# Row sums on one core: one contiguous run of 105 rows per partition in place of eight blocks of 16

## The chip, the core and the metric

The kernel runs on one core of a Trainium2 chip. The metric is device time in microseconds (us) of one execution; lower is better. Two engines compute here: VectorE (DVE in the profile) and ScalarE (ACT). SyncE (SP) issues the loads and the last store, ScalarE the other store. The data moves on the core's 16 DMA engines.

## The reference

```python
batch, seq, dim = 32, 512, 1024
x = np.random.randn(batch, seq, dim).astype(np.float32)
out = np.sum(x, axis=-1).astype(np.float32)      # (32, 512)
```

There are 16,384 rows of 1,024 floats (4 KB each). 67.1 MB are read, 64 KB are written, and every element is used in one addition.

## The kernel before

The rows are spread over 128 partitions, 128 rows to each. They are cut into eight blocks of 2,048 rows; in a block, partition p holds 16 neighbouring rows (64 KB), so a block is one contiguous stretch of 8 MB, and a partition's 64 KB follow those of the partition before it. `sums` is a tile of 128 x 128 floats that gathers one sum for each row: column g*16 + q is row q of block g.

The order of work is written out by hand (`manual_schedule`); each engine runs its own list in program order, with semaphore waits between the engines. All loads are issued by SP into tiles of a pool with three buffers (`inpool`), so a load waits until the tile three before it has been read. `rows` issues a load and the work on it: either one reduction of all its rows on VectorE (`vec`, L141), or row by row, some on VectorE (`halves`, L155: one half of the row is added to the other with a running sum) and some on ScalarE (`act`, L168: a copy with a running sum into PSUM).

1. The first load takes the first 7 rows (28 KB) per partition of the last block. It is moved by `issue_first_load_at_entry` to the program's entry, ahead of the barrier that starts the engines.
2. Blocks 0 to 6 follow, each one load of 16 rows (64 KB per partition, 8 MB in all). Blocks 0 to 5 are reduced by one VectorE instruction each. Block 6 is split: 9 rows to VectorE and 7 to ScalarE. The load of block 1 is held by hand until the reduction of the first 7 rows is done ("no descriptors of later loads while the first ones start").
3. The rest of the last block comes in loads of 6 rows, 2 rows, and the last row in two pieces of 536 and 488 elements (L222, L223).
4. Two stores (L191): `sums` of blocks 0 to 6 from ScalarE's queue, held until the load of two rows has landed, and the 16 sums of the last block from SP's queue at the very end. In the first one every partition writes seven pieces of 64 bytes, in the second one piece of 64 bytes.
5. `wait_for_the_store_at_the_clear` lets the last store run beside the barrier at the end; only GpSimd's clearing of the semaphores waits for it. `order_waits` arranges which of several waits an instruction itself carries.

Of the kernel before, what the change touches and what calls it, by code (L numbers as in the profile page):

```python
# [100 lines left out]
@with_exitstack  # L101
def kernel(
    ctx: ExitStack,
    tc: tile.TileContext,
    x: bass.AP,
    out: bass.AP,
):
    nc = tc.nc
    nc.at_finalize(issue_first_load_at_entry)
    nc.at_finalize(order_waits)  # L110
    nc.at_finalize(wait_for_the_store_at_the_clear)
    fp32 = mybir.dt.float32
    P = 128
    batch, seq, dim = x.shape
    rows = batch * seq
    J = rows // P
    BIG = 16


    x_g = x.flatten_outer_dims().rearrange("(g p j) d -> g p j d", p=P, j=BIG)  # L120
    out_v = out.rearrange("b s -> (b s)").rearrange("(g p j) -> p g j", p=P, j=BIG)

    def rows_from(j, n):
        return x_g[j // BIG, :, j % BIG : j % BIG + n, :]

    last = J // BIG - 1
    FIRST = 7
    pieces = (536, 488)  # L130

    with (
        tc.tile_pool(name="in", bufs=3) as inpool,
        tc.tile_pool(name="unread", bufs=4, space=bass.MemoryType.PSUM) as upool,
        tc.tile_pool(name="stage", bufs=1) as stpool,
        tc.manual_schedule(),
    ):
        sums = stpool.tile([P, J], fp32)

        def vec(dst, src):  # L140
            return nc.vector.tensor_reduce(  # L141
                out=dst, in_=src, axis=mybir.AxisListType.X, op=mybir.AluOpType.add
            )

        def hold(inst, until, reason):
            tc.add_manual_dep(
                inst.ins,
                until.ins.name,
                mybir.DependencyInfo(mybir.DependencyClass.Sync, mybir.DependencyReason.DATA),
                reason=reason,  # L150
            )

        def halves(dst, src):
            n = src.shape[-1] // 2
            return nc.vector.tensor_tensor_reduce(  # L155
                out=src[:, :n],
                in0=src[:, :n],
                in1=src[:, n:],
                scale=1.0,
                scalar=0.0,  # L160
                op0=mybir.AluOpType.add,
                op1=mybir.AluOpType.add,
                accum_out=dst,
            )

        def act(dst, src, n):
            unread = upool.tile([P, dim], fp32)
            nc.scalar.activation(  # L168
                out=unread[:, :n],
                in_=src,  # L170
                func=mybir.ActivationFunctionType.Copy,
                accum_out=dst,
            )

        sums_of = []

        def rows(t, a, n, j, n_act, pairs=False):
            nv = n - n_act
            block = t[:, a * dim : (a + n) * dim].rearrange("p (n d) -> p n d", d=dim)
            load = nc.sync.dma_start(out=block, in_=rows_from(j, n))  # L180
            if pairs:
                for q in range(nv):
                    sums_of.append(halves(sums[:, j + q : j + q + 1], block[:, q, :]))
            else:
                sums_of.append(vec(sums[:, j : j + nv], block[:, :nv, :]))
            for q in range(nv, n):
                act(sums[:, j + q : j + q + 1], block[:, q, :], dim)
            return load

        def store(eng, g0, g1):  # L190
            return eng.dma_start(  # L191
                out=out_v[:, g0:g1],
                in_=sums[:, g0 * BIG : g1 * BIG].rearrange("p (g j) -> p g j", j=BIG),
            )


        j = last * BIG
        t = inpool.tile([P, BIG * dim + 4], fp32)
        rows(t, 0, FIRST, j, 0)
        first = sums_of[-1]  # L200
        for g in range(last):
            t = inpool.tile([P, BIG * dim + 4], fp32)
            if g < last - 1:
                load = rows(t, 0, BIG, g * BIG, 0)
            else:
                rows(t, 0, BIG, g * BIG, 7, pairs=True)
            if g == 1:
                hold(load, first, "no descriptors of later loads while the first ones start")

        t = inpool.tile([P, BIG * dim + 4], fp32)  # L210
        rows(t, FIRST, 6, j + FIRST, 2, pairs=True)
        two = rows(t, FIRST + 6, 2, j + FIRST + 6, 1, pairs=True)
        a = BIG - 1

        j += a
        c, width = pieces
        whole = t[:, a * dim + c : BIG * dim + 2]
        nc.vector.memset(whole[:, width + 1 :], 0.0)  # L220
        part = t[:, a * dim : a * dim + c]
        nc.sync.dma_start(out=part, in_=rows_from(j, 1)[:, 0, :c])  # L222
        nc.sync.dma_start(out=whole[:, 1 : width + 1], in_=rows_from(j, 1)[:, 0, c:])  # L223
        hold(store(nc.scalar, 0, last), two, "its packets come behind those of the loads")
        halves(whole[:, :1], part)
        halves(sums[:, j : j + 1], whole)
        store(nc.sync, last, last + 1)


# [28 lines left out]
```

## Time and profile before

| | before |
|---|---|
| median of 3 runs | 161.61 us (161.48 to 161.74) |
| span of the profiled execution | 160.3 us, 1.3 us less than the median; its own whole time is not listed apart from the runs, and the median stands for it |
| VectorE busy | 120.6 us (75%), 40 instructions |
| ScalarE busy | 11.9 us (7%), 21 instructions |
| DMA, SP's queue (q1) | 1,872 packets, 67.12 MB, 97.7% of 16 engines' span |
| DMA, ScalarE's queue (q10) | 912 packets, 0.06 MB, 0.4% |
| mean rate over the span | 419 GB/s |

Busy time is the time in which an engine executes; its share is of the span. A DMA packet is one piece that one DMA engine moves, here one partition's contiguous bytes of one load or store, and each DMA adds 16 small ones that raise its semaphore. The share of a queue is the time that its packets took, as a share of 16 engines over the span.

### The profile page before, as it was taken

What the parts mean: (1) busy time and instruction counts of PE and PEld (TensorE: products, weight loads), DVE (VectorE), ACT (ScalarE), POOL (GpSimd) and SP (SyncE); (2) the same over time, 40 slices, a digit from 0 to 9 for tenths busy, and PEclk for the clock granted to TensorE, in tenths of its full rate; (3) what the DMA queues carried; (4) which work ended last, traced back from release to release, by engine and by line L of the source; (5) the groups of instructions that cost most, each with busy time, mean ns of one, the idle gap of its engine ahead of it and who ended that gap; (6) DMA issues with size and microseconds to landing.
All of it is one profiled execution on the core that took longest, in us unless ns stands there. A gap on an engine that the chain in (4) does not pass through costs nothing.

```text
span 160.3 us, 132 instructions
## 1 busy us (share of the span) xinstructions
DVE 120.6 (75%) x40; ACT 11.9 (7%) x21; POOL 0.2 (0%) x4
## 2 busy tenths in 40 slices
DVE  0029600499986999679995999949999499994955
ACT  3000000000000000000000000000000000003993
POOL 0000000000000000000000000000000000000000
DMA  8999999899799699699699699796996996996994
GB/s 300 386 491 523 392 392 523 376 409 523 327 458 523 294 491 523 262 523 523 262 523 523 262 523 441 343 523 278 507 523 262 523 523 262 523 523 264 423 384 123
DMA packets 2784, 67.18 MB, mean 419 GB/s; under 512 B 1248, under 2 KB 1376, under 8 KB 1504
## 3 DMA queue, kind: packets, MB, share of 16 engines
q1 hardware_dynamic: 1872, 67.12, 97.7%
q10 hardware_dynamic: 912, 0.06, 0.4%
HBM read 67.11 MB, written 0.07 MB: 419 GB/s over the span
## 4 chain that ended last, share of the span: by engine, by line
DMA 71%; DVE 27%; SPq 1%; issue 0%; DVEq 0%
DMA t<-in_x_dram 71%; DVE sums L141 26%; SPq L180 0%; SPq L222 0%; DVE t L155 0%; DVEq L253 0%
## 5 line engine op out<-in xcount | busy, mean ns | idle before, releaser
L141 DVE TENSOR_REDUCE sums<-t 128x16 f32<-128x16384 f32 (+1 forms) x7 | 110.9, 15848 | 33.8 <-DMA t<-in_x_dram 33.8
L168 ACT ACTIVATE unread<-t 128x1024 f32<-128x1024 f32 x10 | 10.1, 1012 | 145.3 <-DMA t<-in_x_dram 145.3
L155 DVE CUSTOM_DVE_ANT_0 t<-t 128x512 f32<-128x512 f32 (+2 forms) x16 | 9.6, 656 | 4.1 <-DMA t<-in_x_dram 4.0
L168 ACT ACTIVATION_READ_ACCUMULATOR unread<-t 128x1 f32 x10 | 1.9, 187 | 0.0
L168 ACT ACT_TABLE_LOAD x1 | 1.3, 1283 | 0.8 <-PEq L242 0.8
L155 DVE DVE_READ_ACCUMULATOR2_ANT sums<- 128x1 f32 x15 | 1.3, 84 | 0.0
L242 POOL MEMSET const-bfloat16-1.0<- 128x1 bf16 x1 | 0.1, 101 | 0.0
L242 POOL MEMSET const-uint8-127<- 128x1 uint8 x1 | 0.1, 101 | 0.0
L242 POOL MEMSET const-float32-0.0<- 128x1 f32 x1 | 0.1, 98 | 0.2 <-issue 0.2
L242 POOL MEMSET const-float32-1.0<- 128x1 f32 x1 | 0.1, 98 | 0.0
L155 DVE DVE_READ_ACCUMULATOR2_ANT t<- 128x1 f32 x1 | 0.1, 83 | 0.0
L220 DVE MEMSET t<- 128x1 f32 x1 | 0.1, 59 | 0.0
## 6 DMA issues: line engine op xcount, KB each, us to landing
t<-in_x_dram SPq DMA_DIRECT2D x1, 3584.0 KB, 11.0
t<-in_x_dram SPq DMA_DIRECT2D x1, 3072.0 KB, 29.0
t<-in_x_dram SPq DMA_DIRECT2D x1, 1024.0 KB, 31.1
t<-in_x_dram SPq DMA_DIRECT2D x1, 268.0 KB, 31.4
t<-in_x_dram SPq DMA_DIRECT2D x1, 244.0 KB, 31.4
t<-in_x_dram SPq DMA_DIRECT2D x7, 41.1
out_dram<-sums ACTq DMA_DIRECT2D x1, 56.0 KB, 2.1
out_dram<-sums SPq DMA_DIRECT2D x1, 8.0 KB, 1.4
```

What stands on the lines that cost most here:

```text
L141: return nc.vector.tensor_reduce(out=dst, in_=src, axis=mybir.AxisListType.X, op=mybir.AluOpType.add)
L155: return nc.vector.tensor_tensor_reduce(out=src[:, :n], in0=src[:, :n], in1=src[:, n:], scale=1.0, scalar=0.0, op0=mybir.AluOpType.add, op ...
L168: nc.scalar.activation(out=unread[:, :n], in_=src, func=mybir.ActivationFunctionType.Copy, accum_out=dst,)
L220: nc.vector.memset(whole[:, width + 1 :], 0.0)
L242: nc = _bacc.Bacc("TRN2", target_bir_lowering=False, num_devices=1)
```

## The change

The rows are assigned to partitions in another way, and the loads, the stores and one wait change with it. Each partition now holds 7 rows of a first block (rows 0 to 895 of x), 105 neighbouring rows of a second one (420 KB per partition) and 16 rows of a last block. The 105 rows come in seven loads of 15 rows (60 KB per partition), which start 420 KB apart from one partition to the next. The last block is unchanged in shape, but all of its 16 rows are loaded at the end, in loads of 7, 6, 2 rows and the two pieces of the last row. Each block has a store of its own: 28 bytes per partition after the first reduction, from ScalarE's queue; 420 bytes per partition, held as before until the load of two rows has landed; and 64 bytes per partition at the end. The hold on the second large load is gone.

```diff
-    BIG = 16
-    x_g = x.flatten_outer_dims().rearrange("(g p j) d -> g p j d", p=P, j=BIG)
-    out_v = out.rearrange("b s -> (b s)").rearrange("(g p j) -> p g j", p=P, j=BIG)
+    HEAD, BIG, LOADS = 7, 15, 7
+    RUN = BIG * LOADS
+    LAST = J - HEAD - RUN          # 16
+    def block(first, n):
+        lo, hi = first * P, (first + n) * P
+        return (
+            x_r[lo:hi, :].rearrange("(p j) d -> p j d", j=n),
+            out_r[lo:hi].rearrange("(p j) -> p j", j=n),
+        )
+    x_h, out_h = block(0, HEAD)
+    x_m, out_m = block(HEAD, RUN)
+    x_l, out_l = block(HEAD + RUN, LAST)
...
-        rows(t, 0, FIRST, j, 0)                      # j = 112: part of the last block
-        first = sums_of[-1]
-        for g in range(last):
-            t = inpool.tile([P, BIG * dim + 4], fp32)
-            if g < last - 1:
-                load = rows(t, 0, BIG, g * BIG, 0)
+        rows(t, 0, x_h, 0, 0)
+        nc.scalar.dma_start(out=out_h, in_=sums[:, :HEAD])
+        for g in range(LOADS):
+            t = inpool.tile([P, size], fp32)
+            src = x_m[:, g * BIG : (g + 1) * BIG, :]
+            if g < LOADS - 1:
+                rows(t, 0, src, HEAD + g * BIG, 0)
             else:
-                rows(t, 0, BIG, g * BIG, 7, pairs=True)
-            if g == 1:
-                hold(load, first, "no descriptors of later loads while the first ones start")
+                rows(t, 0, src, HEAD + g * BIG, 7, pairs=True)
...
-        rows(t, FIRST, 6, j + FIRST, 2, pairs=True)
-        two = rows(t, FIRST + 6, 2, j + FIRST + 6, 1, pairs=True)
+        rows(t, 0, x_l[:, :7, :], j, 3, pairs=True)
+        rows(t, 7, x_l[:, 7:13, :], j + 7, 2, pairs=True)
+        two, _ = rows(t, 13, x_l[:, 13:15, :], j + 13, 1, pairs=True)
...
-        hold(store(nc.scalar, 0, last), two, "its packets come behind those of the loads")
+        early = nc.scalar.dma_start(out=out_m, in_=sums[:, HEAD : HEAD + RUN])
+        hold(early, two, "its packets come behind those of the loads")
...
-        store(nc.sync, last, last + 1)
+        nc.sync.dma_start(out=out_l, in_=sums[:, j:])
```

In the instruction lists this gives SP one more load; ScalarE one more store, which stands ahead of its table load and all its activations, and 13 activations for 10; VectorE one reduction of 7 and six of 15 rows (for six of 16), and 19 `halves` for 16.

More of the change, by code (lines that the diff above doesn't have):

```diff
@@ L116 @@
     J = rows // P
-    BIG = 16
-    x_g = x.flatten_outer_dims().rearrange("(g p j) d -> g p j d", p=P, j=BIG)
-    out_v = out.rearrange("b s -> (b s)").rearrange("(g p j) -> p g j", p=P, j=BIG)
[L123 to L129, printed above, removed]
+    HEAD, BIG, LOADS = 7, 15, 7
+    RUN = BIG * LOADS
+    LAST = J - HEAD - RUN
+    assert LAST == 16
+    x_r = x.flatten_outer_dims()
+    out_r = out.rearrange("b s -> (b s)")
+    def block(first, n):
[7 more added lines that the diff above has]
+    x_l, out_l = block(HEAD + RUN, LAST)
     pieces = (536, 488)
@@ L173, in act, with rows @@
             )
-        sums_of = []
-        def rows(t, a, n, j, n_act, pairs=False):
+        def rows(t, a, src, j, n_act, pairs=False):
+            n = src.shape[1]
             nv = n - n_act
-            block = t[:, a * dim : (a + n) * dim].rearrange("p (n d) -> p n d", d=dim)
-            load = nc.sync.dma_start(out=block, in_=rows_from(j, n))
+            part = t[:, a * dim : (a + n) * dim].rearrange("p (n d) -> p n d", d=dim)
+            load = nc.sync.dma_start(out=part, in_=src)
@@ L181, in rows @@
             if pairs:
                 for q in range(nv):
-                    sums_of.append(halves(sums[:, j + q : j + q + 1], block[:, q, :]))
+                    done = halves(sums[:, j + q : j + q + 1], part[:, q, :])
             else:
-                sums_of.append(vec(sums[:, j : j + nv], block[:, :nv, :]))
+                done = vec(sums[:, j : j + nv], part[:, :nv, :])
             for q in range(nv, n):
-                act(sums[:, j + q : j + q + 1], block[:, q, :], dim)
-            return load
@@ L190, in store @@
[L190 to L197, printed above, removed]
-        t = inpool.tile([P, BIG * dim + 4], fp32)
-        rows(t, 0, FIRST, j, 0)
-        first = sums_of[-1]
-        for g in range(last):
-            t = inpool.tile([P, BIG * dim + 4], fp32)
-            if g < last - 1:
-                load = rows(t, 0, BIG, g * BIG, 0)
-            else:
-                rows(t, 0, BIG, g * BIG, 7, pairs=True)
-            if g == 1:
-                hold(load, first, "no descriptors of later loads while the first ones start")
@@ L210 @@
-        t = inpool.tile([P, BIG * dim + 4], fp32)
-        rows(t, FIRST, 6, j + FIRST, 2, pairs=True)
-        two = rows(t, FIRST + 6, 2, j + FIRST + 6, 1, pairs=True)
-        a = BIG - 1
-        j += a
+                act(sums[:, j + q : j + q + 1], part[:, q, :], dim)
+            return load, done
+        size = LAST * dim + 4
+        t = inpool.tile([P, size], fp32)
+        rows(t, 0, x_h, 0, 0)
+        nc.scalar.dma_start(out=out_h, in_=sums[:, :HEAD])
+        for g in range(LOADS):
+            t = inpool.tile([P, size], fp32)
+            src = x_m[:, g * BIG : (g + 1) * BIG, :]
+            if g < LOADS - 1:
+                rows(t, 0, src, HEAD + g * BIG, 0)
+            else:
+                rows(t, 0, src, HEAD + g * BIG, 7, pairs=True)
@@ L218 @@
+        j = HEAD + RUN
+        t = inpool.tile([P, size], fp32)
+        rows(t, 0, x_l[:, :7, :], j, 3, pairs=True)
+        rows(t, 7, x_l[:, 7:13, :], j + 7, 2, pairs=True)
+        two, _ = rows(t, 13, x_l[:, 13:15, :], j + 13, 1, pairs=True)
         c, width = pieces
-        whole = t[:, a * dim + c : BIG * dim + 2]
+        a = LAST - 1
+        whole = t[:, a * dim + c : LAST * dim + 2]
         nc.vector.memset(whole[:, width + 1 :], 0.0)
         part = t[:, a * dim : a * dim + c]
-        nc.sync.dma_start(out=part, in_=rows_from(j, 1)[:, 0, :c])
@@ L223 @@
-        nc.sync.dma_start(out=whole[:, 1 : width + 1], in_=rows_from(j, 1)[:, 0, c:])
-        hold(store(nc.scalar, 0, last), two, "its packets come behind those of the loads")
+        nc.sync.dma_start(out=part, in_=x_l[:, a, :c])
+        nc.sync.dma_start(out=whole[:, 1 : width + 1], in_=x_l[:, a, c:])
+        early = nc.scalar.dma_start(out=out_m, in_=sums[:, HEAD : HEAD + RUN])
+        hold(early, two, "its packets come behind those of the loads")
         halves(whole[:, :1], part)
-        halves(sums[:, j : j + 1], whole)
@@ L227 @@
-        store(nc.sync, last, last + 1)
+        halves(sums[:, J - 1 : J], whole)
+        nc.sync.dma_start(out=out_l, in_=sums[:, j:])
 _INS = ['x']
```

## The prediction

> **What bounds the kernel now.** I read the chain that ended last first. It is this, with start, length and what ran:
>
> ```profile
> 0.00 11.00 DMA t<-in_x_dram
> 11.02 7.63 DVE sums L141
> 18.67 31.00 DMA t<-in_x_dram
> ...
> 66.94 41.09 DMA t<-in_x_dram
> 108.05 17.23 DVE sums L141
> ...
> 126.65 31.45 DMA t<-in_x_dram
> 158.13 0.42 DVE t L155
> ```
>
> The VectorE pieces in it are not a bound. The chain follows each load back to what released its issue, but every load was issued while earlier ones still ran: issued at 66.94, landed at 108.03, 41.09 us for bytes that need 19.5. What is to be seen is that it begins with DMA and ends with DMA and 2.2 us of tail. The waits confirm it: VectorE has only loads to wait for.
>
> ```profile
> DVE sums L141 <- DMA t<-in_x_dram: 33.8, 7, 11.7
> DVE t L155 <- DMA t<-in_x_dram: 4.0, 2, 2.3
> ```
>
> Then the groups by shape (count; busy us, mean ns):
>
> ```profile
> L141 DVE TENSOR_REDUCE sums<-t 128x16 f32<-128x16384 f32 x6 | 103.3, 17220 | 22.8 <-DMA t<-in_x_dram 22.8
> L141 DVE TENSOR_REDUCE sums<-t 128x7 f32<-128x7168 f32 x1 | 7.6, 7619 | 11.0 <-DMA t<-in_x_dram 11.0
> ```
>
> A reduction (17.22) is shorter than the 19.3 to 19.5 between landings. Last the windows from landing to landing; the last two columns are DMA share and GB/s:
>
> ```profile
> 11.02:30.34 19.32, 7.62 (x1) 0.00 (x0) 0.00 (x0) 1.00 1.00 434
> 30.34:49.69 19.35, 17.22 (x2) 0.00 (x0) 0.00 (x0) 1.00 1.00 434
> 49.69:69.05 19.36, 17.22 (x2) 0.00 (x0) 0.00 (x0) 1.00 1.00 433
> 69.05:88.54 19.49, 17.22 (x1) 0.00 (x0) 0.00 (x0) 1.00 1.00 430
> 88.54:108.05 19.51, 17.22 (x2) 0.00 (x0) 0.00 (x0) 1.00 1.01 430
> 108.05:127.53 19.48, 17.22 (x1) 0.00 (x0) 0.00 (x0) 1.00 1.00 431
> ```
>
> The 16 DMA engines are full from about 1 us to the end. The time is their start, 4.19 MB for each engine, and the tail; only what lengthens or shortens that stream counts.
>
> The trace's packet records (read one by one, not through a view) give the price of the stream. An undisturbed 64 KB packet takes 2,418 ns, one of 24 KB 912, one of 8 KB 309: 37.7 ns per 1,024 bytes, and 7.7 ns per packet on top. Eight 64 KB packets and a semaphore packet of 9 ns are 19.35 us, the second and third window above. The last four large loads took 0.14, 0.16, 0.13 and 0.18 us more (19.49, 19.51, 19.48, and 147.06 - 127.53 = 19.53): 0.6 us of slow packets, up to 170 ns each, in the first half of each load. At the start, the first packets begin between 0.99 and 1.95 us, and most of them take 1.50 to 1.86 us where later ones of 28 KB take 1.06.
>
> **The change, part by part,** against the profiled execution: span 160.3 us, and 1.3 us around it up to the median of 161.61, which I leave as they are.
>
> *Bytes and packets.* Each engine reads the same 4.19 MB. There is one load more: 8 packets of 7.7 ns and 9 ns, +0.07 us. A 15-row load is eight packets of 2,418 - 4 x 37.7 = 2,267 ns: 18.15 us per load.
>
> *VectorE and ScalarE.* A 15-row reduction is 7,619 + 8 x (17,220 - 7,619)/9 = 16,150 ns, under 18.15, so VectorE still waits 2.0 us for each load. After the last large load it has 8 rows of 0.61 (nine took 147.06 to 152.57): 4.9 us; ScalarE 7 rows, 7.3 us (147.06 to 154.35). The next load, 7 rows, takes 8 x 1,062 ns = 8.5 us, so both finish first; its 4 and 3 rows (2.5 and 3.1 us) lie within the 7.3 us of the 6-row load. From there on the tail is the one before. Cost zero; without that cover the sixteenth row would push ScalarE by 1.03.
>
> *Buffers and queues.* The third large load waits for the first reduction (18.65), with two loads of 18.15 still queued. The loads of the last block wait for the fifth 15-row reduction: landing 11.0 + 5 x 18.15 = 101.8, end 117.9, while the stream is in the sixth load (to 119.9) and has the seventh behind it. Margin 20 us, cost zero. On ScalarE the new store waits at the head of the queue until 18.65; behind it are the table load (1.28 us, at 0.76 before) and the activations, the first at about 138: zero.
>
> *The first store* is new in the middle of the stream: 8 packets of 28 bytes and one for the semaphore on each engine. The nearest row is q10's: 912 packets, 0.4% of 160.3 us, so 57 per engine in 0.64 us, 11.2 ns each: 9 x 11.2 = 0.10 us. Those ran behind one another with no load between them. The far end: each of the eight stops its engine for as long as a load's last packet takes to become a landing, 0.40 us (157.69 to 158.09 in the records): 3.2 us. The lower end is zero. I take 0.10, the row for small stores. The Trainium skill (DMA: Bandwidth & Descriptors, "Queues, rings and completion order") has an engine alternate between queues packet by packet; no row here shows two queues at once. If a store packet then waits for a load packet each time, the store lands some 18 us late, which nobody waits for, and the sum would be the same.
>
> *The second store* has 128 packets of 420 bytes for 896 of 64. Its old packets ran from 157.87 to 158.60 by the records; the last load's had ended at 157.69, and those of the last store began at 159.43. It stood between the two and touched neither, so I give no gain; at most 0.2 us if it slows the last store's landing.
>
> *The hold removed.* The second large load is issued at about 1.1 us, not at 18.67, behind two issues of 0.36 and 0.33. It brings nothing, since the queue never ran dry. Issues in mid-stream cost nothing that the windows show (lower bound 0). At the start three engines began 0.3 to 0.6 us after the other thirteen, when the first large load was being issued; one more such pause would be +0.3. Or a gain of 0.1, if more is in flight. I take the middle of 0 and 0.3: +0.15.
>
> *The addresses.* This is the large unknown. The 16 engines read 60 KB pieces 420 KB apart instead of one solid 8 MB. Lower bound: the slow packets vanish, -0.6. Upper bound: all seven loads show the worst first packets (170 ns) on every packet: 56 x 0.17 = 9.5 us, unlikely in whole; a plausible end is that all seven run twice as slow as the four slow ones, 7 x 0.3 - 0.6 = +1.5. The nearest rows (434 to 430) are within 1% of each other, so I take zero. The Trainium skill (same page, "Latency and other measured facts", HBM row pitch) reports full rate again where a large power-of-two pitch is padded by 4 KB, or where tiles lie contiguously. The change gives up the second remedy, and 420 KB is no power of two; by the rule its sum would be zero too, or -0.6 if 64 KB steps are what slows the four loads.
>
> Sum: 0.07 + 0.10 + 0.15 = +0.32, 161.93, slightly over 0.2%.
>
> **Rivals.** *The slow packets go away.* Place: the four windows of 19.48 to 19.53. For it: they are slow only in half of each load, which looks like addresses, and the 24 KB and 8 KB packets have none. Against: the first three windows have the same layout and are fast. -0.6 + 0.32 gives 161.33; with no start cost 161.18. It decides as soon as more than half of the 0.6 goes.
> *The wide pitch is slower.* For it: every load now touches the whole 55 MB rather than 8 MB. Against: the solid blocks show no cost at new 8 MB stretches. At +0.3 to +1.5: 162.2 to 163.4, middle 162.7.
> *The first store stalls the engines.* 8 packets at 0.05 to 0.2 us beyond their price: 162.3 to 163.5, middle 162.7. Only the second and third landing would be late.
> *Nothing happens:* start and store are hidden, +0.07, 161.68.
>
> **How the numbers follow.** Small costs as summed: 0.37; slow packets gone: 0.25; pitch 0.20; store 0.08; nothing 0.10. About 0.2% (0.32 us, so 161.29 to 161.93) is what a measurement of this kernel can tell from no change. The first case lies on that edge: 0.26 of it slower, 0.11 same. The second: 0.23 faster, 0.02 same. The pitch and the store: 0.28 slower. Nothing: 0.08 same, 0.02 faster. Faster 0.25, same 0.21, slower 0.54. The range reaches from the second case to the middle of the third and fourth: 161.15 to 162.8; the first case's own range is 161.7 to 162.3.
>
> **What would show it.** Right: landings 18.15 to 18.3 us apart at 430 to 434 GB/s, the first at 11.0 to 11.3, the tail after the last landing 2.2 us, a span near 160.6. The first rival shows as seven windows all at 434. The third as windows all under 428; the fourth as one or two slow windows after 18.7 only. I am wrong altogether if VectorE or ScalarE is late after the last large load, if the tail shrinks by more than 0.2, or if the first landing moves by more than 0.5.

## The result and the profile after

| | before | after |
|---|---|---|
| median time | 161.55 us (6 runs, 161.43 to 161.86) | 162.18 us (6 runs, 162.04 to 162.26) |
| span, median of the runs | 159.9 us (76 runs of all comparisons) | 160.0 us |
| time less span, mean | 1.78 us (the same 76 runs) | 2.17 us |

The ratio is 1.0034, 95% interval [1.0021, 1.0046]; a second comparison (b0 below) gave 162.29 against 161.62, 1.0042 [1.0030, 1.0054]. The changed kernel is 0.6 us slower.

The third row of the table is the main finding. Each run lists its time and its span, and they differ by a constant of the kernel, with a scatter of about 0.03 us. The change lengthens the span a little and the time around it by 0.4 us. The page shown for before (160.3 us) is of an execution longer than most: of the 76 runs listed, 6 have a span of 160.3 or more. The 1.3 us that the prediction took to lie around the span was that profile's span set against the median of other runs.

The windows of the profile after, from landing to landing (busy times; then granted clock, DMA share, GB/s):

```profile
0.00:11.13 11.13, 0.00 (x0) 0.00 (x0) 0.20 (x4) 1.00 1.03 418
11.13:29.31 18.18, 7.62 (x2) 1.28 (x1) 0.00 (x0) 1.00 1.00 433
29.31:47.43 18.12, 16.15 (x1) 0.00 (x0) 0.00 (x0) 1.00 1.00 434
47.43:65.60 18.17, 16.18 (x2) 0.00 (x0) 0.00 (x0) 1.00 1.00 433
65.60:83.70 18.10, 16.13 (x1) 0.00 (x0) 0.00 (x0) 1.00 1.00 434
83.70:101.86 18.16, 16.15 (x2) 0.00 (x0) 0.00 (x0) 1.00 1.00 433
101.86:120.00 18.14, 16.15 (x1) 0.00 (x0) 0.00 (x0) 1.00 1.00 434
...
157.87:160.08 2.21, 0.42 (x2) 0.00 (x0) 0.00 (x0) 1.00 0.04 4
```

The large loads run at full rate, 18.1 to 18.2 us each as costed, and the tail of 2.2 us is the old one. Only the first landing is later: the first reduction starts at 11.13 for 11.02. The waits and the groups show that VectorE still waits for loads alone:

```profile
DVE sums L148 <- DMA t<-in_x_dram: 31.6, 7, 11.1
DVE t L162 <- DMA t<-in_x_dram: 10.4, 3, 4.8
```

```profile
L148 DVE TENSOR_REDUCE sums<-t 128x15 f32<-128x15360 f32 x6 | 96.9, 16153 | 20.5 <-DMA t<-in_x_dram 20.5
```

The reduction is the predicted 16.15 us. Nothing in the page explains 0.6 us; its span is even 0.2 shorter than that of the page before. The one row that turned out to matter is VectorE's count of instructions, in the busy times of the pages, here of before and of after:

```profile
DVE 120.6 (75%) x40; ACT 11.9 (7%) x21; POOL 0.2 (0%) x4
```

```profile
DVE 116.1 (73%) x46; ACT 15.2 (10%) x27; POOL 0.2 (0%) x4
```

### The profile page after: what moved, and what is told of

The parts are those of the page before. It is cut to its first block, busy times and chain, and to the rows that moved or that the text cites. A ratio compares the mean times of both kernels' runs of the same rounds, so it can differ in the third digit from the quotient of the medians.

```text
span 160.1 us, 148 instructions
## 1 busy us (share of the span) xinstructions
DVE 116.1 (73%) x46; ACT 15.2 (10%) x27; POOL 0.2 (0%) x4
## 4 chain that ended last, share of the span: by engine, by line
DMA 76%; DVE 20%; SPq 1%; issue 0%; DVEq 0%
DMA t<-in_x_dram 76%; DVE sums L148 20%; SPq L186 1%; SPq L224 0%; DVE t L162 0%; DVEq L256 0%
## 5 line engine op out<-in xcount | busy, mean ns | idle before, releaser
L148 DVE TENSOR_REDUCE sums<-t 128x15 f32<-128x15360 f32 (+1 forms) x7 | 104.5, 14934 | 31.6 <-DMA t<-in_x_dram 31.6
L175 ACT ACTIVATE unread<-t 128x1024 f32<-128x1024 f32 x13 | 13.2, 1013 | 123.3 <-DMA t<-in_x_dram 123.3
L162 DVE CUSTOM_DVE_ANT_0 t<-t 128x512 f32<-128x512 f32 (+2 forms) x19 | 11.5, 661 | 10.6 <-DMA t<-in_x_dram 10.4
L175 ACT ACTIVATION_READ_ACCUMULATOR unread<-t 128x1 f32 x13 | 2.4, 186 | 0.0
## 6 DMA issues: line engine op xcount, KB each, us to landing
out_dram<-sums ACTq DMA_DIRECT2D x1, 3.5 KB, 21.8
```

Of the source, the lines that this page charges most:

```text
L148: return nc.vector.tensor_reduce(out=dst, in_=src, axis=mybir.AxisListType.X, op=mybir.AluOpType.add)
L162: return nc.vector.tensor_tensor_reduce(out=src[:, :n], in0=src[:, :n], in1=src[:, n:], scale=1.0, scalar=0.0, op0=mybir.AluOpType.add, op ...
L175: nc.scalar.activation(out=unread[:, :n], in_=src, func=mybir.ActivationFunctionType.Copy, accum_out=dst,)
```

## The experiments

Every experiment was timed in five rounds beside the kernel before. "Around" is the time less the span, the mean over the runs; spans are medians.

| experiment | VectorE instructions on the page | time | span | around | ratio to before, 95% |
|---|---|---|---|---|---|
| a1 after, first store left out | 46 | 162.34 | 160.15 | 2.18 | 1.0041 [1.0027, 1.0055] |
| a2 after, first store at the end | 46 | 162.77 | 160.55 | 2.21 | 1.0071 [1.0058, 1.0083] |
| a3 after, fewer VectorE instructions | 24 | 162.00 | 160.2 | 1.80 | 1.0020 [1.0011, 1.0029] |
| a4 before, one more store | 40 | 161.58 | 159.8 | 1.78 | 0.9999 [0.9990, 1.0008] |
| b0 after, again | 46 | 162.29 | 160.1 | 2.19 | 1.0042 [1.0030, 1.0054] |
| b1 after, with the hold | 46 | 162.34 | 160.15 | 2.19 | 1.0048 [1.0036, 1.0061] |
| b2 before, without the hold | 40 | 161.62 | 159.8 | 1.80 | 1.0010 [0.9998, 1.0022] |
| b3 before, 6 more on VectorE | 46 | 162.09 | 159.9 | 2.20 | 1.0028 [1.0018, 1.0039] |
| c1 before, contiguous first block | 40 | 161.87 | 160.1 | 1.80 | 1.0010 [1.0000, 1.0020] |
| c2 before, run of 112 rows | 40 | 161.54 | 159.8 | 1.79 | 0.9988 [0.9979, 0.9997] |
| c3 after, 7 fewer on VectorE | 39 | 161.89 | 160.1 | 1.78 | 1.0016 [1.0007, 1.0025] |
| c4 before, 3 more on VectorE | 43 | 161.82 | 160.0 | 1.79 | 1.0005 [0.9994, 1.0017] |

### What lies around the span: stores or instruction lists

**a1.** The first store taken out.

```diff
-        nc.scalar.dma_start(out=out_h, in_=sums[:, :HEAD])
```

> The changed kernel without the store of the first 7 sums: 896 of the 16,384 outputs are left out. The profile after the change has a span of 160.1 us, 0.2 us less than before, and yet the time is 0.6 us longer: time less span went from 1.3 to 2.1 us. Theory A (a third store costs outside the span): time less span back to about 1.3, time 161.3. Theory B (the longer instruction lists cost outside the span): 2.1 as after, 162.1. The prediction's own price for this store, 0.10 us inside the span: span 160.0, time 162.1.

The time stayed at 162.34, around at 2.18. Theory A falls. Of the 0.10 us for this store in the stream nothing shows, since the span is not shorter than b0's 160.1; but the spans are listed in steps of 0.1 us, so these runs can't exclude it.

**a2.** The first store moved to the end.

```diff
-        nc.scalar.dma_start(out=out_h, in_=sums[:, :HEAD])
...
+        head = nc.scalar.dma_start(out=out_h, in_=sums[:, :HEAD])
+        hold(head, two, "its packets come behind those of the loads")
         early = nc.scalar.dma_start(out=out_m, in_=sums[:, HEAD : HEAD + RUN])
```

> The changed kernel with its first store moved to the end of ScalarE's queue, just ahead of the store of 105 sums; the same number of stores and instructions. Theory A (the number of stores): 162.2, time less span 2.1. Theory A2 (a store in the middle of the load stream, or ScalarE's table load behind it, is what costs): time less span 1.3, time 161.4. Theory B (instruction lists): 162.2.

Around stayed at 2.21, so theory A2 falls as well. No theory expected the longer span. It comes from the last store. The rows are its issues, with KB and us to landing, in a2:

```profile
out_dram<-sums ACTq DMA_DIRECT2D x1, 52.5 KB, 2.3
out_dram<-sums ACTq DMA_DIRECT2D x1, 3.5 KB, 1.5
out_dram<-sums SPq DMA_DIRECT2D x1, 8.0 KB, 2.2
```

and in b0, where the 28-byte store goes out early:

```profile
out_dram<-sums ACTq DMA_DIRECT2D x1, 52.5 KB, 1.7
out_dram<-sums ACTq DMA_DIRECT2D x1, 3.5 KB, 21.8
out_dram<-sums SPq DMA_DIRECT2D x1, 8.0 KB, 1.4
```

With three stores close together the last one lands 0.8 us later. The early store of b0 takes 21.8 us to land, but nobody waits for it. The Trainium skill (DMA: Bandwidth & Descriptors, "Queues, rings and completion order") says that an engine alternates between its queues packet by packet; after's packet records agree: the 28-byte packets start between 23.7 and 38.0 us, in eight groups of 16, of which all but one start 2.1 to 2.3 us after the group before, and a load packet takes 2.27 us.

**a3.** VectorE's 8 rows of the last 15-row load and 4 rows of the 7-row load, by one instruction each.

```diff
-                rows(t, 0, src, HEAD + g * BIG, 7, pairs=True)
+                rows(t, 0, src, HEAD + g * BIG, 7)
...
-        rows(t, 0, x_l[:, :7, :], j, 3, pairs=True)
+        rows(t, 0, x_l[:, :7, :], j, 3)
```

> The changed kernel with VectorE's rows of the last 15-row load (8) and of the 7-row load (4) reduced by one instruction each instead of row by row: 22 instructions fewer on VectorE, the same work. One reduction of 8 rows is about 8.7 us for 4.9, of 4 rows 4.4 for 2.5, both within the next load (8.5 and 7.3 us) but for 0.2. Theory B (instruction lists, VectorE's): time less span 1.3, time 161.4 to 161.6. Theories A and A2: 2.1, 162.2.

Around falls by 0.4 us to 1.80, as theory B says; that is the 1.78 of the kernel before, and not the 1.3 that the expectation took over from the prediction. So the time was 162.00, not 161.4 to 161.6: the span did not fall.

**a4.** One more store in the kernel before.

```diff
         first = sums_of[-1]
+        nc.scalar.dma_start(out=out_v[:, last, :FIRST], in_=sums[:, j : j + FIRST])
...
-        store(nc.sync, last, last + 1)
+        nc.sync.dma_start(out=out_v[:, last, FIRST:], in_=sums[:, last * BIG + FIRST :])
```

> The kernel before with one more store: its first 7 sums per partition (28 bytes) are stored from ScalarE's queue after the first reduction, and the last store has 36 bytes instead of 64. One instruction more. Theory A and A2: time less span from 1.3 to 2.1, time 162.4. Theory B (instruction lists): 161.6. The prediction's own price, 0.10 us in the stream: 161.7.

161.58 against 161.63: an additional store of 28 bytes in mid-stream costs nothing that shows, around the span or inside it (the interval leaves room for some 0.15 us either way). Its profile is also a better picture of the layout before than the page first shown. The reductions, start and length:

```profile
30.35 17.22 DVE L141 TENSOR_REDUCE sums<-t 128x16 f32<-128x16384 f32 x1 [11.74 <-DMA t<-in_x_dram]
...
88.38 17.22 DVE L141 TENSOR_REDUCE sums<-t 128x16 f32<-128x16384 f32 x1 [2.13 <-DMA t<-in_x_dram]
107.73 17.22 DVE L141 TENSOR_REDUCE sums<-t 128x16 f32<-128x16384 f32 x1 [2.13 <-DMA t<-in_x_dram]
127.08 17.22 DVE L141 TENSOR_REDUCE sums<-t 128x16 f32<-128x16384 f32 x1 [2.13 <-DMA t<-in_x_dram]
```

127.08 - 107.73 = 19.35, with the same addresses that took 19.48 in the page before. So the same addresses have slow packets in some executions and not in others.

The packet records of all the profiles show more. Count the packets that take over 30 ns more than the usual one, in the first six large loads (768 packets). In the profiles of before, b3, c4, b2 and a4, which have the solid blocks behind the old first load, there are 123, 86, 42, 12 and 3, and the spans fall in the same order: 160.3, 160.1, 160.0, 159.9 and 159.7 us. In the eight profiles with the wide pitch (after, its six variants and c2) there is at most one. c1, with solid blocks behind a contiguous first load, has none. The slow packets thus vary between executions of kernels with the same large loads, and with the wide pitch there were next to none.

### The start, and VectorE's list by itself

**b0.** The changed kernel again.

> The changed kernel itself, again, beside the next three on one chip. All theories: 162.2, span 160.0, time less span 2.17 (the first four experiments gave 1.79 for the kernel before, in 23 runs).

As expected.

**b1.** The hold put back.

```diff
+            if g == 1:
+                hold(load, first, "no descriptors of later loads while the first ones start")
```

> The changed kernel with the hold on its second large load put back. Start theory (the issue of that load in the first 2 us delays the first packets of some engine, and each engine has a fixed share of the bytes, so the delay stays to the end): the slowest of the first packets ends 0.2 to 0.6 us earlier, span 159.7, time 161.9; time less span 2.17 as before the edit. Rival (the hold is worth nothing; the first packets vary with the addresses): span 160.0, time 162.2.

162.34 and a span of 160.15, against 162.29 and 160.1: the start theory, whose hold had been the largest term of the prediction, falls. The slowest of the first 16 packets ends at 3.47 us here and at 3.60 in b0, 0.1 us apart and not the 0.2 to 0.6 that the theory asks for.

**b2.** The hold taken out of the kernel before (the same two lines removed).

> The kernel before without its hold, nothing else. Start theory: span 0.2 to 0.4 longer, 160.1, time 161.9. Rival (the hold is worth nothing): 161.6. Time less span 1.79 in both.

161.62, the same as before. In this kernel the hold has no measured effect with either layout, though b2's interval, up to 1.0022, would by itself leave room for 0.3 us.

**b3.** Six fills on VectorE, long before they could delay anything.

```diff
+        spare = stpool.tile([P, 8], fp32)
+        for q in range(6):
+            nc.vector.memset(spare[:, q : q + 1], 0.0)
```

> The kernel before with six one-column fills of a spare tile at the start of VectorE's list, in the 10 us in which it waits for the first load: as many instructions on VectorE as the changed kernel has. Theory B (VectorE's instruction list costs outside the span): time less span from 1.79 to 2.17, span unchanged at 159.8, time 162.0. Rival (the later instructions of the list near its end matter, or the stores): 1.79, time 161.6.

Around is 2.20, with the span within 0.1 us of where it was. In the timeline of b3 the six fills are one row of 0.20 us, ten us ahead of the first work:

```profile
0.84 0.20 DVE L141 MEMSET spare<- 128x1 f32 x6 [0.84 <-PEq L245]
10.95 7.62 DVE L144 TENSOR_REDUCE sums<-t 128x7 f32<-128x7168 f32 x1 [9.90 <-DMA t<-in_x_dram]
```

So 0.42 us of 162.09 are due to six instructions that delay no work in the profile. ScalarE's list is that of the kernel before, as the page's busy times show:

```profile
DVE 120.8 (75%) x46; ACT 11.9 (7%) x21; POOL 0.2 (0%) x4
```

Lengthening VectorE's list alone does it.

### The addresses, and where the step is

**c1.** The contiguous first block put into the kernel before, with a4's store.

```diff
+    xl = x.flatten_outer_dims()[P * (J - BIG) :, :]
...
+    x_7 = xl[: P * 7, :].rearrange("(p j) d -> p j d", j=7)
+    x_9 = xl[P * 7 :, :].rearrange("(p j) d -> p j d", j=9)
...
     def rows_from(j, n):
+        if j >= J - BIG:
+            q = j - (J - BIG)
+            return x_7[:, q : q + n, :] if q < 7 else x_9[:, q - 7 : q - 7 + n, :]
...
+        nc.scalar.dma_start(out=out_7, in_=sums[:, j : j + FIRST])
...
-        store(nc.sync, last, last + 1)
+        nc.sync.dma_start(out=out_9, in_=sums[:, last * BIG + FIRST :])
```

> The kernel before with its last block assigned otherwise: the first load reads 7 rows per partition from one contiguous stretch of 896 rows (28 KB from one partition to the next, as in the changed kernel) instead of 7 of 16 rows (64 KB apart); the 9 other rows come from the rest of the block; a store of 28 bytes after the first reduction as in the changed kernel. All large loads as before. First-block theory (the contiguous first block starts slower): first landing 11.3 instead of 11.0, span 160.1, time 161.9. Rival (the first packets are slowed by the wide pitch of the large load queued behind): landing 11.0, span 159.8, time 161.6. Time less span 1.79 in both.

The first landing came at 11.76 in its profile, the span was 160.1 and the time 161.87, 0.2 over the kernel before and with an interval that just reaches 1. (The profiled run is c1's longest, 162.34.) The first-block theory holds, against the rival, by the landing; the time alone would not decide it. Start and length of the first piece of the chain in c1:

```profile
0.00 11.76 DMA t<-in_x_dram
```

and in c2:

```profile
0.00 10.94 DMA t<-in_x_dram
```

**c2.** The wide pitch alone: 112 neighbouring rows per partition, in seven loads of 16.

```diff
+    RUN = J - BIG
+    x_m = x.flatten_outer_dims()[: P * RUN, :].rearrange("(p j) d -> p j d", j=RUN)
...
     def rows_from(j, n):
+        if j < RUN:
+            return x_m[:, j : j + n, :]
...
-        hold(store(nc.scalar, 0, last), two, "its packets come behind those of the loads")
+        hold(nc.scalar.dma_start(out=out_m, in_=sums[:, :RUN]), two, "its packets come behind those of the loads")
```

> The kernel before with its seven large blocks as one run of 112 neighbouring rows per partition (448 KB pitch, loads of 16 rows), and one store of 448 bytes per partition for them; first load, hold, last block and instruction lists as before. First-block theory: first landing 11.0, span 159.8, time 161.6; if the wide pitch also spares the slow packets of the large loads, 159.6 and 161.4. Rival (the wide pitch slows the first packets): landing 11.3, span 160.1, time 161.9.

The first landing is at 10.94, and the time is 161.54 in eleven runs that lie within 161.45 to 161.62; the kernel before had 161.44 to 162.18 beside it. The ratio is 0.9988 [0.9979, 0.9997]: the version that beats both kernels, by 0.1%, less than what I had set as measurable at the start. What it gains is that none of its runs was among the longer ones, while 20 of the 33 beside it were longer than its longest. If its times were drawn from the same lot, its eleven would all lie among the shortest 24 of 44 once in some 3,000 draws (an estimate from these runs), so luck is unlikely; and the slow packets, which its profile and the others with the wide pitch lack, are what would lengthen the others. That the pitch is the reason is still argued: c1's profile has none either, without the wide pitch. The skill's row on row pitch (the same page, "Latency and other measured facts") reports losses at pitches that are large powers of two and the full rate again with 4 KB of padding, and it advises contiguous tiles without a rate for them; the pitches here are no powers of two, and the large loads show no such loss, with 433 to 434 GB/s at 420 KB (after) and at 448 KB (c2).

**c3.** The changed kernel, with four VectorE rows by one instruction.

```diff
-        rows(t, 0, x_l[:, :7, :], j, 3, pairs=True)
+        rows(t, 0, x_l[:, :7, :], j, 3)
```

> The changed kernel with the four VectorE rows of its 7-row load reduced by one instruction (4.4 us for 2.5, within the 7.3 us of the next load): 7 instructions fewer on VectorE, one fewer than the kernel before. Theory B: time less span 1.79, span 160.1 as the changed kernel, time 161.9. Rival: 2.18, 162.3.

Around is 1.78 and the time 161.89: seven instructions fewer give the changed kernel back 0.4 us, though VectorE is busy longer. ScalarE's list stays at 27:

```profile
DVE 118.0 (74%) x39; ACT 15.2 (10%) x27; POOL 0.2 (0%) x4
```

What remains is 0.23 us to the kernel before, about as much as in c1. To c2, which also has the wide pitch but the old first block, it is 0.35 us.

**c4.** As b3, with three fills.

> The kernel before with three one-column fills on VectorE at the start instead of six. If the cost outside the span is a step at some length of the list: time less span 1.79 or 2.18, time 161.6 or 162.0. If it grows with every instruction: 1.99, time 161.8.

Around is 1.79. It is a step: nothing up to 43 instructions on the page, 0.4 us at 46. The time, 161.82, is not clearly different from before; eleven runs hold several of the longer spans.

## Why the prediction was right, and where its steps were wrong

The forecast was slower by 0.32 us, 161.93; measured was 162.18, slower, inside the range. The sum came near by luck: its largest term isn't seen in any run, the other two are too small for these runs to tell, and the causes that were found stood in it at nothing. Of the prediction's signs, the spacing of the landings, the first landing and the tail came out; the span near 160.6 did not (160.0).

- **"1.3 us around it ... which I leave as they are": the step that failed.** It holds 0.4 of the 0.6 us. Around was 1.78 before and 2.17 after, and b3, c3 and c4 show that VectorE's three additional rows by `halves` (two instructions each, so 46 for 40) are the whole of it. I had counted these instructions, but priced only their 0.61 us a row, as hidden; that part was right.
- **The hold, +0.15: nothing seen** (b1, b2). The late starters at 1.66 to 1.95 us were read correctly, but one issue more does not add to them: in after the last of the 16 starts at 1.77 us.
- **The first store, +0.10: nothing seen, and too small for these runs to tell** (a1, a4). By after's records its packets take 9 ns each, 0.08 us for the nine of an engine, so the price was of the right size. The rival of stalled engines (0.4 us and more) falls.
- **The addresses, zero.** For the large loads this was nearly right; the cost in "every load now touches the whole 55 MB" isn't there (c2 is 0.1 us faster). What I did not consider is the first block: there the change goes from a pitch of 64 KB to one of 28, and in the packet records the slowest of the first 16 packets ends at 3.05 to 3.18 us in the six profiles with 64 KB and at 3.34 to 4.00 in the eight with 28. The two groups do not overlap. The late start stays to the end: the four profiles a4, after, b0 and c1, which have hardly any slow packets, end this packet at 3.14, 3.36, 3.60 and 4.00 us and have spans of 159.7, 160.1, 160.2 and 160.6. The price is 0.2 us by c1 against the kernel before, and 0.35 by c3 against c2.
- **The rival that the slow packets go away had little to win, but it was not empty.** Its sign came: six windows at 433 to 434 GB/s. But the 0.6 us was read from one of the longer executions; a4, with the same addresses, runs at 19.35 us per load, and the median span of the 76 runs is 0.1 us over c2's. c2's gain over the kernel before, 0.1 us (0.05 to 0.3 by its interval), is the measure that these runs give of it.
- **The eight extra packets, +0.07,** were not measured by themselves.
- **Buffers, VectorE, ScalarE and the tail** went as costed: 16.15 us per reduction, a longest wait of 4.8 us for rows in the end phase, 2.2 us after the last landing. The second store of 420 bytes brought no gain.
- **Two slips of arithmetic** changed nothing: 0.32 us is slightly under 0.2% of 161.61, not over, and the middles of the two slow rivals' ranges are 162.8 and 162.9, not 162.7.

Added up: 0.4 around the span and 0.2 net inside it. By c3 against c2 and c2 against before, the 0.2 would be 0.35 lost at the start and 0.1 won in the large loads (an estimate from these three medians).

## What to carry to other kernels

A profile shows one execution, perhaps one of the longer ones, and only its span. Before pricing an edit, set the span of several runs against their times: here two thirds of the loss lay where no view looks, and "time less span" found it at once. Where a stream of loads never pauses, look at the first packets: what the slowest lost there came back at the end here (0.9 us later in c1 than in a4, and a span longer by 0.9). When an edit adds instructions to a list, compare with a version that adds the same number of idle ones.

## What was not expected of the hardware

Six one-column fills on VectorE, ended 10 us before the first work, made the execution 0.42 us longer outside the recorded span; three made it no longer, and a list of 24 instead of 40 made it no shorter (1.80 and 1.78). ScalarE's list had grown too (27 for 21), but a3 and c3 keep that and show 1.80 and 1.78. What happens in these 0.4 us wasn't shown: no view reaches there, and whether the step lies at a size of the list or at a total with what surrounds the kernel was not tried.

A first load from one contiguous stretch (28 KB from partition to partition) landed 0.1 to 0.8 us later than one of the same size from rows 64 KB apart (the first reduction starts at 11.13 to 11.79 us in eight profiles against 10.95 to 11.06 in six). Why the closer addresses start more slowly stays open.

The solid 8 MB blocks behind the old first load showed between 3 and 123 slow packets from one execution to the next, the wide pitch none or one, and solid blocks behind a contiguous first load none in the one profile there is. Why is open too.
